# Order of the last products and of row tiles' turns, weight-block sums by accumulating transfers, and a bank for each half of the last product

## The chip, the cores and the metric

One core of one Trainium2 chip. The metric is the device time of one launch in microseconds, the median of several runs. TensorE (PE) multiplies, VectorE (DVE), ScalarE (ACT) and GpSimd (POOL) do the elementwise work, and transfers (DMA) are issued from SyncE's queue (SP) and from POOL's. Each engine executes its own list of instructions in order and waits on semaphores for the others.

## The reference

A decoder trunk of two layers over 512 tokens of width 1024, in float32:

```python
h = x
mix = gla_mixer(h, ...)                      # gated linear attention, ends in (..) @ gla_w_o, 1024 x 1024
h = layer_norm(ALPHA * h + mix, ln_g[0, 0], ln_b[0, 0])
h = layer_norm(ALPHA * h + relu(h @ mlp_w_up[0])**2 @ mlp_w_down[0], ln_g[0, 1], ln_b[0, 1])   # d_ff 4096
k, v = split(h @ kv_w)
mix = stick_breaking_attention(h @ sb_w_q[0], k, v) @ sb_w_o[0]
h = layer_norm(ALPHA * h + mix, ln_g[1, 0], ln_b[1, 0])
h = layer_norm(ALPHA * h + relu(h @ mlp_w_up[1])**2 @ mlp_w_down[1], ln_g[1, 1], ln_b[1, 1])
```

## The kernel before

**Precision and tiles.** Every float32 matrix is split into a rounded part hi (ScalarE, L70 and L98) and the rest lo (VectorE, L72 and L99), and every product is three matmuls, hi·hi, hi·lo and lo·hi. The 512 tokens are four row tiles of 128; the residual stream is four tiles `h300` to `h303` of 128 x 1024 (`hs`). Activations that are operands lie transposed in tiles `T` of 128 x 4 x 512 (8 buffers), weights in `raw` or `B` (8 buffers) and their splits in `hi` and `lo` (6 each). PSUM has 8 banks, `ps`. A bank that is written by TensorE and read by another engine is handed over as a whole.

**The seven-product stages.** `seven` multiplies a 512 x 1024 by a 1024 x 1024 block with seven half-size products in place of eight (Strassen-Winograd). It is used nine times: for `gla_w_o`, and four times in each MLP's down projection (g = 0, 2, 4, 6, named by the first of two 512-wide strips of d_ff). The left operand has quarters a11, a12, a21, a22 (views of two tiles), the right one b11 to b22, each as two halves `h`. `product` runs the two parts s = 0, 1 of a product (row tile s of the half; 12 matmuls of 512 columns each) and `add` adds a bank to the residual rows on VectorE. The sums on the a side, s1 = a22 - a21 (L332), s2 = -s1 - a11 (L334), a12 = -a12 - s2 (L340) and a21 = a11 - a21 (L341), are VectorE instructions of 1024 elements; b12 and b22 get their sums by a transfer from POOL's queue that adds in flight (`accum_op`), b11 and b21 by VectorE additions (L336 and L343), which overwrite the tile once its first use has been split. After the first products of the list come p3 (with b22 loaded anew), p7 and p4.

**Stages that end in a norm** (`norms=True`): `gla_w_o`, and g = 6 of both MLPs. There `seven` is a generator that gives control back when a row tile has all its sums. For each row tile VectorE takes statistics in pieces (L176), joins them (L180), adds epsilon (L183), POOL raises to the power -1/2 (`rs`, L185), VectorE centres the row (L189); then TensorE transposes it (the turn, L213), ScalarE applies the affine, and hi and lo are taken into the next stage's T tiles. `finish` does this and leaves the turns of the last row tiles to the next stage: `late` runs them in `up(0)`, the first strip of the next MLP, whose columns come in two halves of 256 (row tiles 0 and 1, then 2 and 3), or behind the first row tile of V. In the last stage of the program (`narrow=True`) nothing is turned: `done1` normalises each row tile (L202, L205) and stores it, and the last product, p4 of row tile 3, is made in two halves of 256 columns.

**What sets the order.** A scheduler takes the program as it is written and interleaves the engines' instructions by its own estimate; within an engine the order is then fixed. POOL's queue is in order, too: an accumulating transfer that waits for its tile holds up all that stands behind it there.

## Time and profile before

| | us |
|---|---|
| median of three runs (1152.15 to 1152.98) | 1152.26 |
| the profiled execution | 1151.73 |
| its span, first to last instruction | 1149.8 |
| TensorE busy | 1121.6 (98%) |
| VectorE busy | 821.0 (71%) |
| ScalarE busy | 555.3 (48%) |
| GpSimd busy | 141.9 (12%) |

The granted clock of TensorE was 0.995 over the span. A row of the timeline has the start in us from the span's start, the length in us, engine, line, operation, output and inputs, shape and count; in brackets the idle time of the engine ahead of it and what ended that. Lines are those of the kernel before (the changed kernel's lines are some 10 to 30 further down).

### The profile page before, as it was taken

What the parts mean: (1) busy time and instruction counts of PE and PEld (TensorE: products, weight loads), DVE (VectorE), ACT (ScalarE), POOL (GpSimd) and SP (SyncE); (2) the same over time, 40 slices, a digit from 0 to 9 for tenths busy, and PEclk for the clock granted to TensorE, in tenths of its full rate; (3) what the DMA queues carried; (4) which work ended last, traced back from release to release, by engine and by line L of the source; (5) the groups of instructions that cost most, each with busy time, mean ns of one, the idle gap of its engine ahead of it and who ended that gap; (6) DMA issues with size and microseconds to landing.
All of it is one profiled execution on the core that took longest, in us unless ns stands there. A gap on an engine that the chain in (4) does not pass through costs nothing.

```text
span 1149.8 us, 14087 instructions
## 1 busy us (share of the span) xinstructions
PE 1121.6 (98%) x5401; PEld 927.7 (81%) x5401; DVE 821.0 (71%) x1003; ACT 555.3 (48%) x823; POOL 141.9 (12%) x195
## 2 busy tenths in 40 slices
PE   8999999999999999999999999999999999999994
PEld 7788888798888888888788877778988888888883
DVE  4576648977757847759936878878667578467697
ACT  4454436654533535535725676754435335245360
POOL 1010110020000100100202434330100001001001
PEclk9999999999999999999999999999999999999998
DMA  7441291294670770831334221111945706708302
GB/s 232 127 116 50 75 247 63 75 300 138 170 215 19 199 204 19 217 95 37 110 110 129 58 71 53 58 37 37 298 142 161 224 19 186 209 27 203 90 1 73
DMA packets 97639, 140.73 MB, mean 122 GB/s; under 512 B 11874, under 2 KB 37602, under 8 KB 97572
## 3 DMA queue, kind: packets, MB, share of 16 engines
q1 hardware_dynamic: 87780, 120.96, 33.0%
q0 software_dynamic: 9792, 18.88, 9.3%
q8 instruction: 42, 0.69, 0.3%
q14 instruction: 25, 0.20, 0.1%
HBM read 137.72 MB, written 2.10 MB: 122 GB/s over the span
## 4 chain that ended last, share of the span: by engine, by line
PE 74%; DVE 19%; ACT 3%; issue 2%; POOL 1%; DMA 0%; SPq 0%; DVEq 0%; POOLq 0%; ACTq 0%
PE ps L318 22%; PE ps L93 17%; PE ps L94 16%; PE ps L95 16%; DVE lo L72 4%; DVE r L787 4%; DVE T L99 2%; DVE h L168 2%; ACT wt L802 1%; DVE bst L176 1%; ACT hi L70 1%; POOL rs L185 1%; DVE ps L779 1%; DVE h L189 1%; DVE qs L762 1%
## 5 line engine op out<-in xcount | busy, mean ns | idle before, releaser
L318 PE MATMUL ps<-hi,T 128*128 128x512 f32 (+1 forms) x1016 | 314.8, 389 | 8.2 <-DVE h L366 8.2
L93 PE MATMUL ps<-T,hi 128*128 128x512 f32 (+1 forms) x768 | 288.3, 376 | 1.7 <-ACT T L98 1.7
L94 PE MATMUL ps<-T,hi 128*128 128x512 f32 (+1 forms) x768 | 285.4, 372 | 0.0
L95 PE MATMUL ps<-T,lo 128*128 128x512 f32 (+1 forms) x768 | 285.4, 372 | 0.0
L72 DVE TENSOR_TENSOR lo<-raw,hi 128x1024 fp32r<-128x1024 f32 x134 | 163.0, 1226 | 125.0 <-ACT hi L70 124.1
L70 ACT ACTIVATE hi<-raw 128x1024 fp32r<-128x1024 f32 x134 | 142.7, 1066 | 181.1 <-PE ps L94 67.8
L318 PEld LDWEIGHTS ps<-hi,T 128*128 128x128 f32 x1016 | 191.1, 189 | 47.5 <-DVE h L366 8.4
L318 PE MATMUL ps<-lo,T 128*128 128x512 f32 (+1 forms) x508 | 197.4, 389 | 0.0
L72 DVE TENSOR_TENSOR lo<-B,hi 128x1024 fp32r<-128x1024 f32 x108 | 131.4, 1223 | 89.7 <-ACT hi L70 89.5
L70 ACT ACTIVATE hi<-B 128x1024 fp32r<-128x1024 f32 x108 | 114.2, 1058 | 160.1 <-PE ps L94 78.5
L93 PEld LDWEIGHTS ps<-T,hi 128*128 128x128 f32 x768 | 144.5, 188 | 26.7 <-ACT T L98 2.1
L95 PEld LDWEIGHTS ps<-T,lo 128*128 128x128 f32 x768 | 144.7, 188 | 25.2
L94 PEld LDWEIGHTS ps<-T,hi 128*128 128x128 f32 x768 | 144.8, 189 | 23.4
L318 PEld LDWEIGHTS ps<-lo,T 128*128 128x128 f32 x508 | 96.0, 189 | 19.4
L93 PE MATMUL ps<-hi,T 128*128 128x512 f32 x256 | 103.0, 403 | 0.0
L94 PE MATMUL ps<-lo,T 128*128 128x512 f32 x256 | 100.8, 394 | 0.1
L95 PE MATMUL ps<-hi,T 128*128 128x512 f32 x256 | 100.8, 394 | 0.0
L274 POOL DMA_DIRECT2D B<-in_mlp_w_down_dram x32 | 38.3, 1197 | 464.7 <-DMA B<-in_mlp_w_down_dram 420.5
L168 DVE TENSOR_TENSOR h<-h,ps 128x512 f32<-128x512 f32 x111 | 75.0, 679 | 10.9 <-PE ps L318 7.3
L787 DVE TENSOR_TENSOR_SCAN r<-r,begin 128x512 f32<-128x512 f32 x40 | 66.2, 1662 | 0.2
L788 POOL TENSOR_TENSOR w<-w,r 128x512 f32<-128x512 f32 x40 | 51.4, 1286 | 75.7 <-DVE r L787 60.4
L99 DVE TENSOR_TENSOR T<-s,T 128x1024 fp32r<-128x1024 f32 (+1 forms) x50 | 55.6, 1111 | 2.3 <-ACT T L98 2.3
(165 smaller groups left out, 1184.4 us busy)
## 6 DMA issues: line engine op xcount, KB each, us to landing
raw<-in_mlp_w_up_dram SPq DMA_DIRECT2D x64, 512.0 KB, 4.9
B<-in_mlp_w_down_dram SPq DMA_DIRECT2D x64, 512.0 KB, 5.7
B<-in_mlp_w_down_dram POOLq DMA_DIRECT2D x32, 512.0 KB, 8.7
raw<-in_gla_w_in_dram SPq DMA_DIRECT2D x20, 512.0 KB, 3.9
raw<-in_mlp_w_down_dram SPq DMA_DIRECT2D x16, 512.0 KB, 4.7
raw<-in_kv_w_dram SPq DMA_DIRECT2D x16, 512.0 KB, 4.0
B<-in_gla_w_o_dram SPq DMA_DIRECT2D x8, 512.0 KB, 8.5
raw<-in_sb_w_q_dram SPq DMA_DIRECT2D x8, 512.0 KB, 4.3
```

What stands on the lines that cost most here:

```text
L70: nc.scalar.activation(hi, raw, AF.Copy)
L72: nc.vector.tensor_tensor(lo, raw, hi.bitcast(F32), op=ALU.subtract)
L93: nc.tensor.matmul(ps, lhsT=a[0], rhs=b[0], start=first, stop=False)
L94: nc.tensor.matmul(ps, lhsT=a[0], rhs=b[1], start=False, stop=False)
L95: nc.tensor.matmul(ps, lhsT=a[1], rhs=b[0], start=False, stop=last)
L99: keep(nc.vector.tensor_tensor(lo, ps, hi.bitcast(F32), op=ALU.subtract))
L168: nc.vector.tensor_tensor(h, h, ps, op=op)
L176: nc.vector.bn_stats(out=self.st[:, parts * n + i, :], in_=h)
L274: nc.gpsimd.dma_start(out=to, in_=weights(more[0], h, more[1]), accum_op=ALU.add)
L318: nc.tensor.matmul(banks[s][:, c], lhsT=a(k, s)[x], rhs=b[k][y][:, c], start=opens and (k, x, y) == (0, 0, 0), stop=closes and (k, x, y) = ...
L787: nc.vector.tensor_tensor_scan(down, down, begins[kind][:, ::-1], 1.0, op0=ALU.mult, op1=ALU.max)
L788: nc.gpsimd.tensor_tensor(w, w, r[:, 1:S + 1], op=ALU.mult)
```

## The change

1. `finish` takes the generator itself. In the stages that turn rows, both parts of p3 come first, then both of p7, then both of p4 (before: p3 and p7 of one part, then of the other), and the generator says when a row has its sums (t) and when it is to be turned (~t). `late` is a list with one entry for each row: in `up(0)` row 2 is turned at piece k = 4 and row 3 at k = 5 (both at k = 4 before; where only row 3 is left, it comes at k = 5), and in V row 2 after the first row tile, row 3 after the second.
2. On the a side, a21 becomes a11 - a21 first, and its split for p7 (`seventh`) is made at once and kept; s2 = -a21 - a22, s1 = -s2 - a11 and a12 = -a12 - s2 follow from it. This is so in all nine stages; the number of VectorE instructions stays the same.
3. In the three stages that end in a norm, b11 and b21 get their sums by transfers: two more for each half of b11 and three for each half of b21, ten in a stage, instead of four VectorE additions.
4. In the last stage each half of the last p4 has a bank of its own.

```diff
-    def finish(mm, cols, hs, sp, work, turns=((), (0,), (1,), (2,))):
+    def finish(steps, cols, hs, sp, work):
...
-        for t in range(NT):
-            mm(t)
-            hs[t].stats()
-            hs[t].centre()
-            for q in turns[t]:
-                turn(q, work)
-        rest = [t for t in range(NT) if all(t not in q for q in turns)]
-        return lambda work: [turn(t, work) for t in rest]
+        rest = list(range(NT))
+        for t in steps:
+            if t < 0:
+                turn(~t, work)
+                rest.remove(~t)
+            else:
+                hs[t].stats()
+                hs[t].centre()
+        return [lambda work, t=t: turn(t, work) for t in rest]
...
-        tt(s1, a22, a21, op=ALU.subtract)
+        minus = lambda out, a, b: nc.vector.scalar_tensor_tensor(out, a, -1.0, b, op0=ALU.mult, op1=ALU.subtract)
+        tt(a21, a11, a21, op=ALU.subtract)
+        seventh = split_a(a21)
+        minus(s2, a21, a22)
+        minus(s1, s2, a11)
         third = split_a(s1), split_b(1)
-        nc.vector.scalar_tensor_tensor(s2, s1, -1.0, a11, op0=ALU.mult, op1=ALU.subtract)
-        for b22, b12, b11, b21 in bs:
-            tt(b11, b22, b11, op=ALU.add)
+        for h, (b22, b12, b11, b21) in enumerate(bs):
+            if norms:
+                more(b11, h, 0, 1)
+                more(b11, h, 1, 1)
+            else:
+                tt(b11, b22, b11, op=ALU.add)
...
-        for b22, b12, b11, b21 in bs:
-            tt(b21, b21, b11, op=ALU.add)
+        minus(a12, a12, s2)
+        for h, (b22, b12, b11, b21) in enumerate(bs):
+            if norms:
+                for k, j in ((0, 0), (0, 1), (1, 1)):
+                    more(b21, h, k, j)
+            else:
+                tt(b21, b21, b11, op=ALU.add)
...
-            yield
-            if not narrow:
+            yield s
+        if not narrow:
+            for s in range(2):
                 part(s, *p7, ys, False, False)
                 add(s, ys, 1, 1, last=True)
+                yield ~s
...
-                ps, hrow = bank(), hs[3]
                 for q in range(2):
                     c = slice(256 * q, 256 * q + 256)
-                    part(s, *p4, [None, ps], True, True, c)
+                    ps, h = [None, bank()], hs[3].h[:, c]
+                    part(s, *p4, ps, True, True, c)
...
-                    if g == 0 and (c0, k, f) == (0, 4, 0):
-                        late(work)
+                    if g == 0 and c0 == f == 0 and (k == 5 or k == 4 and len(late) > 1):
+                        late.pop(0)(work)
...
-            if (n, t) == (0, 0):
-                late(chain)
+            if late:
+                late.pop(0)(chain)
```

What this does to the engines' order is seen at three places. The first is VectorE in the last stage, from the first sum of the a side to the third product's split (`T1467` holds s1 and s2, `s21456` a12 and a22, `s21387` a11 and a21; `L99` makes a lo of the a side, `L72` a lo of a weight). Before:

```order
L332 TENSOR_TENSOR T1467_8845<-s21456_8812,s21387_8381 128x4x256
L168 TENSOR_TENSOR h300_1602<-h300_1602,ps1473_8857 128x512
L99 TENSOR_TENSOR T1475_8885<-s21456_8812,T1475_8885 128x4x256
L99 TENSOR_TENSOR T1480_8897<-T1467_8845,T1480_8897 128x4x256
L168 TENSOR_TENSOR h301_1603<-h301_1603,ps1474_8871 128x512
L334 SCALAR_TENSOR_TENSOR T1467_8845<-T1467_8845,s21387_8381 128x4x256
L72 TENSOR_TENSOR lo1491_8948<-B1461_8831,hi1490_8946 128x1024
L168 TENSOR_TENSOR h300_1602<-h300_1602,ps1485_8911 128x512
L99 TENSOR_TENSOR T1489_8943<-T1467_8845,T1489_8943 128x4x256
```

After:

```order
L168 TENSOR_TENSOR h300_1602<-h300_1602,ps1473_8869 128x512
L99 TENSOR_TENSOR T1475_8897<-s21456_8824,T1475_8897 128x4x256
L99 TENSOR_TENSOR T1480_8909<-s21387_8393,T1480_8909 128x4x256
L168 TENSOR_TENSOR h301_1603<-h301_1603,ps1474_8883 128x512
L343 SCALAR_TENSOR_TENSOR T1467_8857<-s21387_8393,s21456_8824 128x4x256
L72 TENSOR_TENSOR lo1492_8966<-B1461_8843,hi1491_8964 128x1024
L343 SCALAR_TENSOR_TENSOR T1467_8857<-T1467_8857,s21387_8393 128x4x256
L168 TENSOR_TENSOR h300_1602<-h300_1602,ps1486_8929 128x512
L72 TENSOR_TENSOR lo1494_8970<-B1465_8853,hi1493_8968 128x1024
L176 BN_STATS bst1487_8943<-h300_1602 128x6
L99 TENSOR_TENSOR T1481_8914<-T1467_8857,T1481_8914 128x4x256
```

The third product's operand was the first of these rows and its split the fourth (`T1480`); now the third row is the seventh product's split (`T1480` of the new program), the operand is made by two sums with a weight's lo between them, and its split (`T1481`) is the last row.

The second place is POOL's queue in that stage, behind the transfers that both kernels have (`B1461` and `B1465` are the halves of b11, `B1462` and `B1466` those of b21). Before:

```order
L274 DMA B1460_8828<-in_mlp_w_down_dram 128x2x512
L274 DMA B1463_8835<-in_mlp_w_down_dram 128x2x512
L274 DMA B1464_8838<-in_mlp_w_down_dram 128x2x512
L185 TENSOR_TENSOR rs1515_9067<-ve1514_9065,mhalf_73 128x1
L185 TENSOR_TENSOR rs1518_9095<-ve1517_9093,mhalf_73 128x1
L185 TENSOR_TENSOR rs1523_9140<-ve1522_9138,mhalf_73 128x1
```

After:

```order
L277 DMA B1464_8850<-in_mlp_w_down_dram 128x2x512
L277 DMA B1461_8843<-in_mlp_w_down_dram 128x2x512
L277 DMA B1465_8853<-in_mlp_w_down_dram 128x2x512
L277 DMA B1461_8843<-in_mlp_w_down_dram 128x2x512
L277 DMA B1465_8853<-in_mlp_w_down_dram 128x2x512
L277 DMA B1462_8845<-in_mlp_w_down_dram 128x2x512 x2
L277 DMA B1466_8855<-in_mlp_w_down_dram 128x2x512
L277 DMA B1462_8845<-in_mlp_w_down_dram 128x2x512
L277 DMA B1466_8855<-in_mlp_w_down_dram 128x2x512 x2
L185 TENSOR_TENSOR rs1515_9085<-ve1514_9083,mhalf_73 128x1
L185 TENSOR_TENSOR rs1518_9113<-ve1517_9111,mhalf_73 128x1
```

Ten transfers have come in ahead of the first row's power; those to one tile wait for one another.

The third place is the end of the program on VectorE, the last row tile. Before, and after:

```order
L366 TENSOR_TENSOR h303_1605<-h303_1605,ps1525_9167 128x256
L176 BN_STATS bst1524_9163<-h303_1605 128x6
L366 TENSOR_TENSOR h303_1605<-h303_1605,ps1525_9167 128x256
L176 BN_STATS bst1524_9163<-h303_1605 128x6
L180 BN_AGGR mv1526_9196<-bst1524_9163 128x2
L183 TENSOR_SCALAR ve1527_9198<-mv1526_9196 128x1
```

```order
L396 TENSOR_TENSOR h303_1605<-h303_1605,ps1525_9185 128x256
L396 TENSOR_TENSOR h303_1605<-h303_1605,ps1526_9200 128x256
L176 BN_STATS bst1524_9181<-h303_1605 128x6 x2
L180 BN_AGGR mv1527_9215<-bst1524_9181 128x2
L183 TENSOR_SCALAR ve1528_9217<-mv1527_9215 128x1
```

The second half has a bank of its own, `ps1526`, and its addition has moved ahead of the first half's statistics.

More of the change, by code (lines that the diff above doesn't have):

```diff
@@ L218, in turn_affine, with by_tiles @@
         put(sp.hi[u][:, :, c], sp.lo[u][:, :, c], y.rearrange("p (a b) -> p a b", a=4))
-    def finish(mm, cols, hs, sp, work, turns=((), (0,), (1,), (2,))):
+    def by_tiles(mm):
+        for t in range(NT):
+            mm(t)
+            yield t
+            if t > 0:
+                yield ~(t - 1)
+    def finish(steps, cols, hs, sp, work):
         def turn(t, work):
@@ L266, in seven, with more @@
         bs = []
+        def more(b, h, k, j):
+            nc.gpsimd.dma_start(out=b.rearrange("p (a b) -> p a b", a=2), in_=weights(k, h, j), accum_op=ALU.add)
         for h in range(2):
             four_b = []
-            for k, j, more in ((1, 1, (0, 1)), (0, 1, (0, 0)), (0, 0, None), (1, 0, None)):
+            for k, j, other in ((1, 1, (0, 1)), (0, 1, (0, 0)), (0, 0, None), (1, 0, None)):
                 b = pool.tile([P, 1024], F32, tag="B", bufs=8, name=nm("B"))
-                to = b.rearrange("p (a b) -> p a b", a=2)
-                nc.sync.dma_start(out=to, in_=weights(k, h, j))
-                if more:
-                    nc.gpsimd.dma_start(out=to, in_=weights(more[0], h, more[1]), accum_op=ALU.add)
+                nc.sync.dma_start(out=b.rearrange("p (a b) -> p a b", a=2), in_=weights(k, h, j))
+                if other:
+                    more(b, h, *other)
                 four_b.append(b)
@@ L349, in seven @@
             add(s, zs, 0, 1, last=True)
[L350 to L351 removed]
+            yield s
+        if not narrow:
+            for s in range(2):
                 part(s, *p7, ys, False, False)
                 add(s, ys, 1, 1, last=True)
+                yield ~s
         for s in range(2):
[L355 to L361 removed]
+            if not narrow:
+                part(s, *p4, ys, False, True)
+                add(s, ys, 1, 0, last=True)
+                yield 2 + s
+                continue
+            part(s, *p7, ys, False, True)
+            add(s, ys, 1, 1, last=True)
+            add(s, ys, 1, 0)
+            ys[s] = None
+            if s == 0:
+                part(s, *p4, ys, True, True)
+                add(s, ys, 1, 0, last=True)
+            else:
                 for q in range(2):
                     c = slice(256 * q, 256 * q + 256)
[L364 to L373 removed]
+                    ps, h = [None, bank()], hs[3].h[:, c]
+                    part(s, *p4, ps, True, True, c)
+                    tt(h, h, ps[1][:, c], op=ALU.add)
+                    hs[3].stat(0, q, h, 2)
+            yield 2 + s
     gl = tc.tile_pool(name="gla", bufs=1, reuse_waits="tile")
@@ L642, in yoco_kernel @@
     hT = Split()
-    late = finish(lambda t: next(steps), vcols, hs, hT, sgs, SEVEN)
+    late = finish(steps, vcols, hs, hT, sgs)
     op.__exit__(None, None, None)
@@ L694, in mlp @@
         steps = down(NG - 2, norms=True, narrow=l == 1)
-        got = done(lambda t: next(steps), work)
+        got = done(steps, work)
         ml.__exit__(None, None, None)
@@ L860, in part2, with done1 @@
             hs[t].add(n, pss[n], False, True)
-    late = finish(part2, vcols, hs, h3T, chain)
+    late = finish(by_tiles(part2), vcols, hs, h3T, chain)
     sbx.__exit__(None, None, None)
-    def done1(mm, work):
+    def done1(steps, work):
         vec = lnvec(1, 1)
@@ L869, in store @@
             nc.sync.dma_start(out=out2[128 * t:128 * t + 128, c], in_=hs[t].h[:, c])
-        for t in range(NT):
-            mm(t)
+        for t in steps:
             hs[t].stats()
```

23 lines of the change are left out of this document (3 added, 20 removed).

## The prediction

> **What bounds the kernel now.** I read the page first, then TensorE's waits, then the timeline at each of them. All times are of one profiled execution: it took 1151.73 us, of which the span is 1149.8; the three timed runs have a median of 1152.26, so a change worked out on the profiled execution is carried over to that median as a difference.
>
> ```profile
> span 1149.8 us, 14087 instructions
> PE 1121.6 (98%) x5401; PEld 927.7 (81%) x5401; DVE 821.0 (71%) x1003; ACT 555.3 (48%) x823; POOL 141.9 (12%) x195
> ...
> PE ps L318 <- DVE h L366: 8.2, 1, 8.2
> PE ps L213 <- DVE h L189: 3.8, 3, 2.0
> PE ps L93 <- ACT T L98: 1.7, 1, 1.7
> ```
>
> TensorE is busy for 98% of the span, and no edit takes a matmul away, so only its waits and the end can pay. The last three rows (total, times, longest) are the waits at places which the diff touches: 13.7 us together. Four of the five instructions behind them are:
>
> ```profile
> 224.60 0.74 PE L93 MATMUL ps<-T,hi 128*128 128x256 f32 x4 [1.67 <-ACT T L98]
> 226.19 0.76 PE L213 MATMUL ps<-ident,h 128*128 128x128 f32 x5 [0.84 <-DVE h L189]
> ...
> 566.97 1.09 PE L213 MATMUL ps<-ident,h 128*128 128x128 f32 x8 [2.01 <-DVE h L189]
> ...
> 809.06 0.66 PE L213 MATMUL ps<-ident,h 128*128 128x128 f32 x4 [0.93 <-DVE h L189]
> ```
>
> The reader is to see in the brackets the wait and its releaser: a row tile's transposes (L213) wait for its centring (L189), or the next matmul waits for a turned row tile (T). The fifth is at the end:
>
> ```profile
> 1130.52 0.28 PE L318 MATMUL ps<-hi,T 128*128 128x256 f32 x1
> 1138.96 0.58 PE L318 MATMUL ps<-hi,T 128*128 128x256 f32 x1 [8.15 <-DVE h L366]
> 1141.47 0.41 PE L318 MATMUL ps<-hi,T 128*128 128x256 f32 x1
> ...
> 1138.49 0.41 DVE L366 TENSOR_TENSOR h<-h,ps 128x256 f32<-128x256 f32 x1
> 1138.94 0.43 DVE L176 BATCH_NORM_STATS2 bst<-h 128x6 f32<-128x256 f32 x1
> 1141.92 0.42 DVE L366 TENSOR_TENSOR h<-h,ps 128x256 f32<-128x256 f32 x1 [2.56 <-PE ps L318]
> 1142.38 0.43 DVE L176 BATCH_NORM_STATS2 bst<-h 128x6 f32<-128x256 f32 x1
> 1142.84 0.26 DVE L180 BATCH_NORM_AGGREGATE mv<-bst 128x2 f32<-128x24 f32 x1
> ...
> 1096.00:1138.00 42.00, 34.80 (x160) 28.88 (x158) 42.00 (x62) 14.36 (x15) 2.76 (x3) 0.97 0.07 26
> ```
>
> The last row is a window by engine (length, then PE, PEld, DVE, ACT and POOL busy): VectorE has worked without a pause for the 42 us ahead of its add at 1138.49. So the 8.15 us on TensorE are not 8.15 us of the end. VectorE itself idles only the 2.56 us in which the second half is multiplied.
>
> **Own banks at the end.** With a bank for each half TensorE runs the second half right behind the first and is done some 1.5 us after 1130.8 (twelve 256-column matmuls, as from 1129.3 to 1130.8), about 6 us before VectorE gets there. VectorE then does add, add, statistics, statistics: four steps of 0.40 to 0.46 us by the rows above, 1.8 us, in place of 1142.84 - 1138.49 = 4.35. Gain 2.5 us; behind it the norm and the stores stay as they are. Bounds: 2.0 (if the second add still waits half a microsecond) to 2.6.
>
> **The turn of row 3 one step later, on the way to MLP 1.** It moves behind 12 matmuls of 256 columns, 12 x 0.12 = 1.4 us, more than the 0.93 it waits. Its centring depends on nothing that moved. Gain 0.9; bounds 0.6 to 0.93, since the second column half needs this row tile's split and comes 0.5 us sooner.
>
> **A longer chain on the a side, in all nine stages.** The third product's operand was one subtraction; now it is the last of three, and the seventh product's split comes ahead of it. In the last stage:
>
> ```profile
> 1096.09 1.23 DVE L332 TENSOR_TENSOR T<-s,s 128x1024 f32<-128x1024 f32 x1
> 1098.96 1.22 DVE L99 TENSOR_TENSOR T<-T,T 128x1024 fp32r<-128x1024 f32 x1
> 1100.10 0.68 DVE L168 TENSOR_TENSOR h<-h,ps 128x512 f32<-128x512 f32 x1
> 1103.57 1.06 ACT L70 ACTIVATE hi<-raw 128x1024 fp32r<-128x1024 f32 x1 [0.56 <-PE ps L318]
> 1104.50 0.62 PE L318 MATMUL ps<-hi,T 128*128 128x512 f32 x2
> 1104.96 0.39 PE L318 MATMUL ps<-lo,T 128*128 128x512 f32 x1
> ```
>
> Before, the sum stood at 1096.09 and its split was done 4.6 us before the third product began (1104.73, the second of the two matmuls of the row at 1104.50). By the new order the sums begin behind the add of 1100.10: sum, a weight's lo, sum, 3 x 1.14 us after 1100.3, is 1103.7. ScalarE is then in the hi of 1103.57, until 1104.6, and has the new hi at 1105.6. The lo follows on VectorE at 1107.2, but eight matmuls that need no lo of the a side stand in between, two of each of four half products, 8 x 0.23 = 1.8 us (0.46 for two by the last rows), which reach to 1107.4. So TensorE waits 0.9 us (0 to 1.9) in each of the three stages that end in a norm. In the last stage that costs nothing at the end: VectorE, which sets it, has one subtraction (1.14 us) fewer behind 1096, because a21's is made before, in idle time, and loses as much by waiting for the third product. In w_o the same count gives 0.9, too.
>
> In the other six stages I cost this at nothing; the cover is this slack:
>
> ```profile
> 383.30 1.22 DVE L99 TENSOR_TENSOR T<-T,T 128x1024 fp32r<-128x1024 f32 x1
> 386.79 0.62 PE L318 MATMUL ps<-hi,T 128*128 128x512 f32 x2
> ```
>
> The third product's split is done at 384.4 and the product starts at 387.0; the first product's T buffer, which the split must now wait for, is free before that. If the cover were gone, it would be up to 1 us for each of six.
>
> **Turns of rows 0 to 2.** These I walked by hand through the new order of both engines, with 1.14 us for a 1024-wide instruction of VectorE, 0.60 for a 512-wide one, 2.72 for a half product (12 x 0.227), 1.0 for eight transposes and 1.5 from a variance to the centring that needs its power:
>
> ```profile
> 225.32 0.81 DVE L189 TENSOR_SCALAR h<-h,mv,rs 128x1024 f32<-128x1024 f32 x1 [0.44 <-POOL rs L185]
> ...
> 235.58 0.68 DVE L195 TENSOR_TENSOR h<-h,lnb 128x512 f32<-128x512 f32 x1
> 236.18 0.68 DVE L99 TENSOR_TENSOR T<-s,T 128x512 fp32r<-128x512 f32 x1
> ```
>
> In w_o, rows 0 and 1 are finished ahead of p7's end and turned ahead of p4, so both gaps of 224.60 and 226.19 (2.5 us) go: I get row 1's centring at 217.1 where TensorE comes at 217.4, and row 2's at 228.9 where it comes at 229.7. Late next are row 3's centring (232.5, in time) and its split for the second column half, 238.5 against 237.9. Sum for w_o: -2.5 + 0.9 + 0.6 = -1.0; bounds -2.2 to +0.5. Before K and V, row 3's turn goes behind another row tile of V (24 x 0.23 = 5.5 us), so 2.0 goes. Against it stand the 0.9 and a new wait: rows 0 and 1 now have their statistics in one piece behind the last splits, row 0's centring ends at 551.8 and TensorE is there at 551.1. Sum -2.0 + 0.9 + 0.7 = -0.4; bounds -1.5 to +1.5. One thing is moved past here: row 3's power on POOL now stands behind the attention's fills.
>
> ```profile
> 564.30 1.38 POOL L185 TENSOR_TENSOR rs<-ve,mhalf 128x1 f32<-128x1 f32 x1
> 565.63 0.73 POOL L718 MEMSET begin<- 128x768 f32 x1
> ...
> 569.31 0.16 POOL L782 MEMSET r<- 128x1 f32 x3
> ```
>
> They take 3.9 us (565.63 to 569.5) and begin with row 1's last split, about 563.2; the power ends at 568.6, the centring at 569.9. TensorE comes at 571.6, so nothing is lost, but of 5.5 us only 1.7 are left.
>
> **Sums by transfers.** Four additions of 1.14 us leave VectorE in each of three stages. In the two MLP stages they stood in its idle time (1076 to 1086), so nothing is gained; in w_o two of them shorten a busy stretch in which it then waits for TensorE. In come 30 transfers, ten a stage, each adding 512 KB to a tile, one behind the other on a tile and all in POOL's order. In the last stage the first may start when the lo of b11 is made, and the last must have landed before the hi of the last b21:
>
> ```profile
> 1075.19 1.22 DVE L72 TENSOR_TENSOR lo<-B,hi 128x1024 fp32r<-128x1024 f32 x1
> 1115.87 1.06 ACT L70 ACTIVATE hi<-B 128x1024 fp32r<-128x1024 f32 x1 [0.30 <-PE ps L318]
> 1120.27 2.35 DVE L72 TENSOR_TENSOR lo<-B,hi 128x1024 fp32r<-128x1024 f32 x2
> ...
> L274 POOL DMA_DIRECT2D B<-in_mlp_w_down_dram x32: 1185/1198/1216, 234.3 to 1059.0; - x32
> B<-in_mlp_w_down_dram POOLq DMA_DIRECT2D x1, 512.0 KB, 5.9
> ...
> B<-in_mlp_w_down_dram POOLq DMA_DIRECT2D x2, 512.0 KB, 7.3
> ...
> B<-in_mlp_w_down_dram POOLq DMA_DIRECT2D x2, 512.0 KB, 9.8
> ...
> 1082.00:1096.00 14.00, 14.00 (x63) 11.59 (x63) 4.74 (x4) 7.83 (x11) 0.00 (x0) 1.00 0.00 0
> ```
>
> In POOL's new order five landings and two issues (1.20 us each) stand behind one another from 1076.3, where b11's second lo ends: 1078.7 + 5D. D, from issue to landing, was 5.9 us for one such transfer by itself (1034 to 1042), 7.3 for two some 2.7 us apart (315 to 329), 9.8 for two among 2.5 MB of loads (1055 to 1070). The chain ends at 1108.2, 1115.2 or 1127.7. The hi must be ready when VectorE reaches the last lo, at 1121.4, so the landing is due by 1120.3: D below 8.3. I take 7.3, because pairs overlap here and, by the last row, nothing else is moved (DMA share 0.00). Cost 0; bounds 0 and 7.4 us in this stage, the same in MLP 0, where the offset between the stages is constant, and in w_o, where three landings stand behind one another from 182.7 and 208 is the due time (D below 8.4), 0 and 4. What hides it is the slack of 5 us; gone, each microsecond is one of the end, as VectorE goes in order.
>
> [...]
>
> **Sum.** -2.5 - 0.9 - 1.0 - 0.4 + 0 = -4.8 us: the profiled execution from 1151.73 to 1146.9, the median from 1152.26 to 1147.5, or 0.42% less.
>
> **Rivals.** Chance in brackets; 0.2% (2.3 us) is what a measurement of this kernel can tell.
> The likeliest (0.55): the sum, 1147.5, own range 1146 to 1149.9.
> The chain of transfers is late (0.22): for it, D = 9.8 is in the same trace; against it, the quiet window. At D = 8.9 the landing is 3 us late in both MLP stages, +6 on the sum, 1153.5; from D = 9.1 (2 x 4 = 8 us, over 4.8 + 2.3 = 7.1) the kernel is slower. Half of it I give to no change, a little under half to slower.
> The new waits are larger (0.18): the third product waits 1.9 us, as it would without the interleaved matmuls, in w_o and MLP 0, and row 0's turn 1.5: +2.8, 1150.3, no change by a little.
> The whole 8.15 us come back (0.05): only if VectorE had slack before 1138.49, which the window excludes; 1142.
>
> Faster 0.65 (0.55, 0.05, and a part of the third), no change 0.24, slower 0.11. The range leaves out the very late chain and the whole 8 us: 1145.3 to 1153.
>
> **What would show it.** At the end TensorE without a wait between the two halves and VectorE's last aggregate about 2.5 us sooner; no wait above 1 us at L213; 0.9 us before the third product in three stages; on VectorE no wait for a hi of b21 near 1120, 544 and 209. A wait of the last lo for its hi, behind a landing, would make me wrong.

## The result and the profile after

The changed kernel takes 1144.39 us (median of four runs, 1143.0 to 1145.03) against 1152.2 before: ratio 0.9933, 95% interval 0.9916 to 0.995. A second series of five runs, beside other runs of the kernel before, gave 1143.94 and 0.9921 (0.9907 to 0.9934). The forecast was 1147.5 and the range began at 1145.3: the direction was right, the gain of 7.8 us was over 60% larger than the 4.8 forecast. One run of "one transfer more" below took 1878 us at a granted clock of 0.655 and is left out of its median.

The first lines to read are again TensorE's waits. In the list of waits (total, times, longest) of the changed kernel the places that the diff touches are now:

```profile
PE ps L329 <- ACT T L98: 2.3, 3, 0.8
...
PE ps L94 <- DVE T L99: 0.4, 1, 0.4
PE ps L213 <- DVE h L189: 0.2, 1, 0.2
```

13.7 us of waits have become 2.9. They stand in these rows of the timeline: the third product in w_o, in MLP 0 and in the last stage (L329 is `part`'s matmul, L318 before), row 3's split for the second column half, and row 1's turn before K and V.

```profile
193.45 0.50 PE L329 MATMUL ps<-hi,T 128*128 128x512 f32 x1 [0.83 <-ACT T L98]
237.12 0.39 PE L94 MATMUL ps<-T,hi 128*128 128x256 f32 x1 [0.38 <-DVE T L99]
526.86 0.50 PE L329 MATMUL ps<-hi,T 128*128 128x512 f32 x1 [0.74 <-ACT T L98]
551.12 0.55 PE L213 MATMUL ps<-ident,h 128*128 128x128 f32 x3 [0.15 <-DVE h L189]
1100.56 0.50 PE L329 MATMUL ps<-hi,T 128*128 128x512 f32 x1 [0.74 <-ACT T L98]
```

The end on VectorE, where before stood two adds 3.4 us apart:

```profile
1132.04 1.54 DVE L205 SCALAR_TENSOR_TENSOR h<-h,rs,lnb 128x512 f32<-128x512 f32 x3
1133.49 0.74 DVE L396 TENSOR_TENSOR h<-h,ps 128x256 f32<-128x256 f32 x2
1134.15 0.74 DVE L176 BATCH_NORM_STATS2 bst<-h 128x6 f32<-128x256 f32 x2
1134.93 0.26 DVE L180 BATCH_NORM_AGGREGATE mv<-bst 128x2 f32<-128x24 f32 x1
```

From the first add to the aggregate it is 1.44 us (1133.49 to 1134.93) in place of 4.35.

All kernels of this study have the same 5401 matmuls, so the start of the n-th one can be compared between two traces. The difference to the first profile of the kernel before is flat inside a stage and steps where something changed; that splits each profiled execution into five parts (us against the kernel before; "start" is up to 190 us, "w_o" 190 to 260, "MLP 0 to V" 500 to 600, "to MLP 1" 780 to 840, "end" from there to the last instruction). Between 260 and 500 nothing moved by more than 0.01 us in any kernel, and between the other parts by 0.1 at most.

| kernel | start | w_o | MLP 0 to V | to MLP 1 | end | median, us | ratio (95%) |
|---|---|---|---|---|---|---|---|
| changed | -1.01 | -1.48 | -1.78 | -0.82 | -3.44 | 1144.39 | 0.9933 (0.9916, 0.995) |
| changed, again | -0.20 | -1.45 | -1.76 | -0.82 | -3.38 | 1143.94 | 0.9921 (0.9907, 0.9934) |
| before, again | -0.09 | +1.15 | +1.62 | 0 | 0 | 1153.02 | 1.0003 (0.9993, 1.0013) |
| before + own banks | -1.64 | +1.03 | 0 | 0 | -2.90 | 1149.87 | 0.9976 (0.9965, 0.9986) |
| one bank | -1.31 | -1.40 | -1.77 | -0.82 | -0.49 | 1146.46 | 0.9946 (0.9932, 0.9959) |
| late turns together | -0.89 | -1.47 | +4.19 | 0 | -3.43 | 1149.35 | 0.9969 (0.9956, 0.9982) |
| products in pairs | -0.46 | -0.80 | -1.47 | -0.84 | -3.44 | 1144.84 | 0.9932 (0.9917, 0.9947) |
| sums on VectorE | -1.23 | -0.94 | -1.80 | -0.84 | -2.80 | 1144.82 | 0.9934 (0.9917, 0.995) |
| a side as before | -2.64 | -0.39 | -2.24 | -0.83 | -3.49 | 1144.01 | 0.9919 (0.9903, 0.9935) |
| third's split first | -0.12 | -0.94 | -2.84 | -0.83 | -3.93 | 1142.64 | 0.991 (0.9893, 0.9927) |
| one transfer more | -1.37 | -1.45 | -1.78 | -0.83 | -1.70 | 1143.53 | 0.9922 (0.9905, 0.9938) |
| third's first, not in w_o | +0.36 | -1.45 | -1.30 | -0.83 | -3.89 | 1142.36 | 0.9914 (0.99, 0.9928) |
| the two combined | -0.55 | -1.45 | -2.83 | -0.83 | -3.99 | 1141.87 | 0.9912 (0.9898, 0.9925) |

The parts behind the start repeat to 0.06 us for the changed kernel, the start itself scatters by 3 us over the fourteen profiles (the first of before stands at 0), and all of that arises in the first 15 us, far ahead of any edit. A median of five runs therefore tells less than the steps do, and below the steps decide. The change's own gain is -1.48 - 1.78 - 0.82 - 3.44 = -7.5 us.

### The profile page after: what moved, and what is told of

It reads as the page before. It is cut to its first block, busy times and chain, and to the rows that moved or that the text cites. A ratio compares the mean times of both kernels' runs of the same rounds, so it can differ in the third digit from the quotient of the medians.

```text
span 1141.3 us, 14137 instructions
## 1 busy us (share of the span) xinstructions
PE 1118.9 (98%) x5401; PEld 925.5 (81%) x5401; DVE 807.3 (71%) x991; ACT 554.5 (49%) x823; POOL 178.2 (16%) x225
## 4 chain that ended last, share of the span: by engine, by line
PE 78%; DVE 15%; ACT 3%; issue 2%; POOL 1%; DMA 0%; SPq 0%; DVEq 0%; POOLq 0%; ACTq 0%
PE ps L329 26%; PE ps L93 17%; PE ps L94 16%; PE ps L95 16%; DVE r L812 4%; DVE lo L72 3%; ACT wt L827 1%; DVE h L168 1%; DVE T L99 1%; DVE h L195 1%; DVE bst L176 1%; DVE ps L804 1%; ACT hi L70 1%; DVE qs L787 1%; POOL rs L185 1%
## 5 line engine op out<-in xcount | busy, mean ns | idle before, releaser
L329 PE MATMUL ps<-hi,T 128*128 128x512 f32 (+1 forms) x1016 | 314.2, 388 | 2.3 <-ACT T L98 2.3
L72 DVE TENSOR_TENSOR lo<-raw,hi 128x1024 fp32r<-128x1024 f32 x134 | 163.8, 1225 | 135.9 <-ACT hi L70 135.4
L329 PEld LDWEIGHTS ps<-hi,T 128*128 128x128 f32 x1016 | 190.2, 188 | 42.7 <-ACT T L98 4.1
L72 DVE TENSOR_TENSOR lo<-B,hi 128x1024 fp32r<-128x1024 f32 x108 | 131.1, 1222 | 93.8 <-ACT hi L70 93.6
L329 PE MATMUL ps<-lo,T 128*128 128x512 f32 (+1 forms) x508 | 196.9, 388 | 0.0
L277 POOL DMA_DIRECT2D B<-in_mlp_w_down_dram x52 | 62.4, 1230 | 539.5 <-DMA B<-in_mlp_w_down_dram 451.3
L329 PEld LDWEIGHTS ps<-lo,T 128*128 128x128 f32 x508 | 95.4, 188 | 19.2
L95 PEld LDWEIGHTS ps<-hi,T 128*128 128x128 f32 x256 | 48.3, 189 | 10.6 <-DVE T L99 0.3
```

The source lines that it names most:

```text
L72: nc.vector.tensor_tensor(lo, raw, hi.bitcast(F32), op=ALU.subtract)
L95: nc.tensor.matmul(ps, lhsT=a[1], rhs=b[0], start=False, stop=last)
L277: nc.gpsimd.dma_start(out=b.rearrange("p (a b) -> p a b", a=2), in_=weights(k, h, j), accum_op=ALU.add)
L329: nc.tensor.matmul(banks[s][:, c], lhsT=a(k, s)[x], rhs=b[k][y][:, c], start=opens and (k, x, y) == (0, 0, 0), stop=closes and (k, x, y) = ...
```

## The experiments

**Own banks alone.** On the kernel before:

```diff
-                ps, hrow = bank(), hs[3]
+                hrow = hs[3]
                 for q in range(2):
-                    c = slice(256 * q, 256 * q + 256)
+                    c, ps = slice(256 * q, 256 * q + 256), bank()
```

> The kernel before with one edit: each half of the last product's last row tile gets a bank of its own. Theory A (VectorE carries the end, and only its detour over TensorE between the two halves can be saved): the second half is multiplied right behind the first, and VectorE goes from its first add to the last aggregate in about 1.45 us in place of 4.35: 2.9 us less than the kernel before, about 1149.3; with 0.6 us more if the last stores also close faster, as in the changed kernel, 1148.7. Rival B (the whole wait of 8.15 us on TensorE comes back): about 1144. Rival C (the end's gain needs the changed kernel's sums too, because VectorE's own work ahead of it must shrink): no change by more than 0.5 us, 1152.

Theory A, to the hundredth: the end is 2.90 us shorter, not 8. The 0.6 us of the stores did not come with it (see the last section). The run also showed something that was not looked for: its w_o, which it shares word for word with the kernel before, took 1.03 us longer. That is taken up under "before, again".

**One bank again.** The changed kernel with this edit undone:

```diff
+                ps = [None, bank()]
                 for q in range(2):
-                    ps, h = [None, bank()], hs[3].h[:, c]
+                    h = hs[3].h[:, c]
```

> The changed kernel with one edit undone: the two halves of the last row tile share one bank again (its add and statistics stay in the new order, add and statistics of the first half ahead of the second half's add as far as the bank forces it). Theory A: the tail alone grows again, from the first half's add to the last aggregate by 2.9 us, all else as in the changed kernel: about 1147.3, that is 4.9 us less than the kernel before. Rival B (TensorE's 8 us wait is what costs): about 1151 to 1152. Rival C (the edits in the order of the a side had moved VectorE's last part too): the first add at another place than 45 us behind the stage's start.

The end grows by 2.95 us, and TensorE's wait returns almost whole:

```profile
1126.38 0.28 PE L329 MATMUL ps<-hi,T 128*128 128x256 f32 x1
1133.83 0.58 PE L329 MATMUL ps<-hi,T 128*128 128x256 f32 x1 [7.17 <-DVE h L397]
```

A wait of 7.17 us on the engine that is busy for 98% of the span is worth 2.9. The add at which VectorE arrives stands 0.1 us from where it stood in the kernel before, counted from the stage's start: rivals B and C fall.

**The a side in the order of before.** The reorder of the sums undone (a21's own difference stands behind a12's sum again, and its split for p7 behind that):

```diff
-        tt(a21, a11, a21, op=ALU.subtract)
-        seventh = split_a(a21)
-        minus(s2, a21, a22)
-        minus(s1, s2, a11)
+        tt(s1, a22, a21, op=ALU.subtract)
         third = split_a(s1), split_b(1)
+        minus(s2, s1, a11)
...
+        tt(a21, a11, a21, op=ALU.subtract)
```

> The changed kernel with the sums of the a side in the order of the kernel before (a22 - a21 first, from it the next; a21's own difference last). Theory A: the third product's waits of 0.84, 0.74 and 0.74 us in the three stages that end in a norm go, since its operand is one subtraction again; of these the ones in w_o and MLP 0 are worth the 1.6 us that they take on TensorE, the last stage's nothing at the end because VectorE carries it, but there a subtraction (1.14 us) comes back into VectorE's busy stretch, +0.3 to +1.1: in sum 0.5 to 1.3 us less than the changed kernel, 1143.1 to 1143.9. Rival B (the new order is what let the row tiles of w_o and MLP 0 be turned without a wait): a wait of about 1 us comes back at the turns of each of both stages, 1145 to 1147. Rival C: in the other six stages something waits, up to 1 us in each.

The third product's waits go in all three stages, as A says. In MLP 0 that is a gain of 0.46, and at the end it is nothing. In w_o rival B holds: 1.09 us are lost against the changed kernel, and the wait is at row 1's operands again:

```profile
221.78 0.74 PE L93 MATMUL ps<-T,hi 128*128 128x256 f32 x4 [1.04 <-ACT T L98]
222.80 0.39 PE L94 MATMUL ps<-T,hi 128*128 128x256 f32 x1 [0.28 <-DVE T L99]
```

By the steps this kernel is 0.6 us worse than the changed one; its median is equal within the scatter of the start.

**The third's split first.** One line moved behind the third's split, `seventh = split_a(a21)`.

> The changed kernel with one line moved: the seventh product's split is made behind the third's, not ahead of it. Theory A: the third product's operand comes one split (1.14 us of VectorE, and its hi on ScalarE) earlier, so its wait of 0.74 to 0.84 us in three stages goes; the seventh is needed much later and waits for nothing; w_o and MLP 0 gain 0.7 to 0.8 us each, the last stage nothing: 1.5 us less than the changed kernel, about 1142.9. Rival B (the third product's wait is set by ScalarE's hi of the weights, not by the a side's chain): the wait stays, 1144.4. Rival C (in the six other stages the third's split must wait for the first product's buffer, that the seventh took before): up to 1 us in each of six, 1146 to 1150.

Theory A in MLP 0 (-1.06 against the changed kernel) and, unlike A, also at the end: the wait is gone, and VectorE reaches the last row tile's add 1.06 us earlier from the stage's start. (0.55 of it is given back in the last stores, see the last section.) In w_o the wait stays, 0.84, as rival B says, but B's reason is not shown. The operand comes no earlier there: its last sum starts at 191.98 (191.09 in the changed kernel, whose start is 0.89 us shorter), since VectorE had made the seventh's split at 179.40, ahead of a wait for TensorE that has now grown from 0.34 to 1.46 us. ScalarE stands in order behind a weight's hi and is free at about the time at which that sum ends, so this does not tell which of the two holds the product up:

```profile
192.19 1.07 ACT L70 ACTIVATE hi<-raw 128x1024 fp32r<-128x1024 f32 x1 [3.00 <-PE ps L329]
193.24 2.96 ACT L98 ACTIVATE T<-T 128x1024 fp32r<-128x1024 f32 x3
194.35 0.50 PE L329 MATMUL ps<-hi,T 128*128 128x512 f32 x1 [0.84 <-ACT T L98]
```

Waits of 0.29 and 0.42 us come in behind it, and w_o loses 0.54. In sum 1.0 us better than the changed kernel. C did not occur.

**Late turns together.** `late` runs all that it holds at the earlier place (piece k = 4, or row tile 0 of V):

```diff
-                    if g == 0 and c0 == f == 0 and (k == 5 or k == 4 and len(late) > 1):
-                        late.pop(0)(work)
+                    if g == 0 and (c0, k, f) == (0, 4, 0):
+                        while late:
+                            late.pop(0)(work)
...
-            if late:
+            while late:
                 late.pop(0)(chain)
```

> The changed kernel with the late turns put back: the turns that were moved one step apart (row 3's behind another row tile, or behind another step) are made together again at the earlier place. Theory A (TensorE is in front of the centring there, and the later turn only covers this wait): the waits of about 2.0 us before K and V and 0.9 us on the way to MLP 1 come back, and perhaps 0.5 in w_o; 2.5 to 3.5 us more than the changed kernel by the stages of its profile, about 1147.2. Rival B (the centring has become early enough through the other edits, since POOL's power of rows 0 and 1 took 0.56 us and not 1.4): less than 1 us comes back, 1144.4 to 1145.4. Rival C (as B before K and V, but A on the way to MLP 1, where nothing else had moved): 0.8 us, 1145.2.

A in kind, but far larger: nothing in w_o, 0.82 on the way to MLP 1, and 5.97 us before K and V, where the kernel before had waited 2.0. TensorE there:

```profile
567.19 1.39 PE L213 MATMUL ps<-ident,h 128*128 128x128 f32 x8 [4.17 <-DVE h L189]
568.23 0.78 PE L93 MATMUL ps<-hi,T 128*128 128x512 f32 x1
568.81 0.63 PE L94 MATMUL ps<-lo,T 128*128 128x512 f32 x1
569.23 0.63 PE L95 MATMUL ps<-hi,T 128*128 128x512 f32 x1
```

A window of 3 us behind the wait, by engine (length, PE, PEld, DVE, ACT and POOL busy, granted clock):

```profile
568.00:571.00 3.00, 3.00 (x10) 2.42 (x9) 2.98 (x6) 3.00 (x9) 0.00 (x0) 0.50 0.16 47
```

4.17 are the wait. The matmuls behind it follow each other by 0.43 us, where the undisturbed ones take 0.227, at a granted clock of 0.50; these make the other 1.8 us. Why 4.17 and not 2.0: this trace is 2.36 us ahead of the kernel before when the stage begins (its start and w_o), and counted from there TensorE is at the turn 0.4 us later (563.0 against 565.0, start less wait), but the centring begins 3.0 us later (566.3 against 565.7). In the new order VectorE makes a weight's lo and row 2's centring between row 3's last add (557.69) and its statistics (560.85); the variance then stands behind another lo that waits for ScalarE, and POOL can only begin behind that:

```profile
563.99 1.23 DVE L72 TENSOR_TENSOR lo<-raw,hi 128x1024 fp32r<-128x1024 f32 x1 [1.23 <-ACT hi L70]
565.13 0.15 DVE L183 TENSOR_SCALAR ve<-mv 128x1 f32<-128x1 f32 x1
...
565.37 0.92 POOL L185 TENSOR_TENSOR rs<-ve,mhalf 128x1 f32<-128x1 f32 x1 [0.15 <-DVE ve L183]
566.32 0.81 DVE L189 TENSOR_SCALAR h<-h,mv,rs 128x1024 f32<-128x1024 f32 x1 [0.45 <-POOL rs L185]
```

**Products in pairs.** p3 and p7 of one part, then of the other, and the turns of rows 0 to 2 where they were, all else as changed:

```diff
             yield s
-        if not narrow:
-            for s in range(2):
+            if not narrow:
+                if s == 1:
+                    yield ~0
                 part(s, *p7, ys, False, False)
                 add(s, ys, 1, 1, last=True)
-                yield ~s
...
                 yield 2 + s
+                if s == 0:
+                    yield ~1
```

> The changed kernel with the last products in pairs by row half again (third and seventh of one row half, then of the other), and the turns of rows 0 to 2 at the places of the kernel before. Theory A (the order of the products is what gives the row tiles their time): in w_o the two waits of 1.67 and 0.85 us return, with the third product's 0.8 kept, so w_o is 1.5 to 2.5 us slower than in the changed kernel; before K and V row 0's statistics come earlier, so its 0.15 us wait goes, but the gap ahead of row 1 and the restarts come back, +0.3 to +1; the last stage is unchanged. In sum 1146.2 to 1147.9. Rival B (the sums by transfers gave VectorE the time in w_o): w_o keeps at least 1 us of its gain of 1.5 us, 1144.4 to 1145.2.

Both theories missed. The waits of 1.67 and 0.85 do not return; waits of 0.47 and 0.61 stand at w_o's turns instead. The order of the products, with the turns that go with it, is worth 0.68 us in w_o and 0.31 before K and V: less than half of w_o's gain, so A is too large, and more than B left to it. That the median lies in B's range is the scatter of medians: by the steps this kernel is 1.0 us worse than the changed one.

**Sums on VectorE.** `tt(b11, b22, b11)` and `tt(b21, b21, b11)` for all stages, and no further transfer that adds.

> The changed kernel with the sums of the weight blocks b11 and b21 on VectorE again in the three stages that end in a norm (four additions of 1.14 us a stage, and no transfer that adds). Theory A (in both MLP stages the additions stand in VectorE's idle time, in w_o partly in a busy stretch): the MLP stages as in the changed kernel to 0.3 us, w_o 0 to 1.2 us longer; 1144.4 to 1145.6. Rival B (the sums by transfers are what lets VectorE reach the last row tiles sooner): VectorE's add of the last row tile comes 2 to 4.6 us later behind the start of the last stage, the span grows by as much, 1146.4 to 1149. Rival C (the transfers cost by their landing or by their issue on POOL): it is faster than the changed kernel by more than 0.5 us, below 1143.9.

Theory A: the MLP stages keep their times (0.02; at the end the add of the last row tile is at the same place to 0.01, and the 0.64 that are lost lie in the last stores). W_o loses 0.54. So 20 of the 30 transfers buy nothing in these runs.

**One transfer more.** To measure the slack of the chain in the last stage:

```diff
-                for k, j in ((0, 0), (0, 1), (1, 1)):
+                for k, j in ((0, 0), (0, 1), (1, 1)) + ((1, 1),) * (narrow and h == 1):
```

> The changed kernel with one adding transfer more (512 KB) on the second half of b21 in the last stage alone, behind the other three on this tile; the sum in this tile is another than the reference's, all else is the same. Theory A (the transfers of one tile follow one another by a landing each, 5.8 to 6.2 us): the last packets end at about 1117 in place of 1111, the hi of that half starts that much later, VectorE waits 1 to 2 us before the last lo, and the end is 1 to 2 us later: 1145.4 to 1146.4. Rival B (the transfers of one queue overlap, so one more costs its packets only, 3.6 us): the landing is at about 1114.5 and nothing waits: 1144.4. Rival C (TensorE waits, too, since the half's products stand in line, 2 to 4 us more at the end): 1147 to 1149.

Theory A, with the wait at the place the prediction had named for a late chain:

```profile
1116.67 1.06 ACT L70 ACTIVATE hi<-B 128x1024 fp32r<-128x1024 f32 x1 [5.50 <-DMA B<-in_mlp_w_down_dram]
...
1117.76 1.22 DVE L72 TENSOR_TENSOR lo<-B,hi 128x1024 fp32r<-128x1024 f32 x1 [1.65 <-ACT hi L70]
```

The end part of the profiled execution is 1.74 us longer than in the changed kernel, and TensorE waits for nothing more. So the chain had some 4.5 us to spare in the last stage: one landing more (6.2 us, the row of the ten transfers further down) is too much by 1.7. (The sum in this tile is wrong by the transfer that was added; the kernel only serves to measure time.) The median does not show this (1143.53); only the profiled execution, at 1144.36, is known to have waited.

**The third's split first, but not in w_o.**

```diff
+        if norms and fresh:
+            seventh = split_a(a21)
         minus(s2, a21, a22)
         minus(s1, s2, a11)
         third = split_a(s1), split_b(1)
-        seventh = split_a(a21)
+        if not (norms and fresh):
+            seventh = split_a(a21)
```

> The changed kernel with the third product's split ahead of the seventh's in eight of the nine stages; w_o keeps the changed kernel's order. Theory A (each stage keeps the gain that it showed by itself: w_o 1.48 us as in the changed kernel against 0.94 with the third first; MLP 0 to the attention 2.84 and the last stage 3.9 as with the third first): 9.1 us less than the kernel before by the stages from w_o on, 0.5 less than with the third first everywhere, 1.5 less than the changed kernel: about 1142.6. Rival B (w_o's 0.5 us between the two orders was the scatter of one profile): w_o as with the third first, 0.94, and a median equal to that kernel's.

W_o as A says (-1.45). But MLP 0, whose instructions are those of the kernel with the third's split first, took 1.54 us longer than there. The last hi of b21, the last lo and row 0's turn tell why:

```profile
543.45 1.06 ACT L70 ACTIVATE hi<-B 128x1024 fp32r<-128x1024 f32 x1 [5.26 <-DMA B<-in_mlp_w_down_dram]
...
544.55 1.22 DVE L72 TENSOR_TENSOR lo<-B,hi 128x1024 fp32r<-128x1024 f32 x1 [1.40 <-ACT hi L70]
...
550.51 1.09 PE L213 MATMUL ps<-ident,h 128*128 128x128 f32 x8 [0.98 <-DVE ve L183]
```

And the transfers of that stage, the ten that add and three plain loads beside them (KB each, median us from issue to landing), of this kernel and then of the one with the third's split first:

```profile
B<-in_mlp_w_down_dram POOLq DMA_DIRECT2D x10, 512.0 KB, 7.5
raw<-in_kv_w_dram SPq DMA_DIRECT2D x3, 512.0 KB, 4.5
```

```profile
B<-in_mlp_w_down_dram POOLq DMA_DIRECT2D x10, 512.0 KB, 6.2
raw<-in_kv_w_dram SPq DMA_DIRECT2D x3, 512.0 KB, 3.7
```

This is the prediction's rival of the late chain, in one execution: all transfers of the stretch landed a fifth later, the hi came after its time, and VectorE passed the delay on to the turns of rows 0 and 1.

**The same two kernels again.**

> The changed kernel unchanged, to have its profile and times a second time beside the others. Theory A (the stages repeat, and only the start differs from run to run): w_o 1.48, MLP 0 to the attention 1.78, the attention 0.82 and the last stage 3.44 us less than in the first profile of the kernel before, each to 0.1 us, while the time up to w_o differs by up to 1 us. Rival B (w_o's gain, too, is a matter of the run): w_o differs by 0.3 us or more.

> The kernel before unchanged, a second profile. [...]

The changed kernel repeats to 0.06 us in each part (A). The kernel before does not: this time w_o is 1.15 and "MLP 0 to V" 1.62 us longer, with the same waits in the same places. The windows behind the two waits, in the second profile and then in the first one (length, busy times, granted clock third from the end):

```profile
226.00:229.00 3.00, 2.91 (x16) 2.84 (x17) 3.00 (x6) 1.33 (x3) 0.00 (x0) 0.64 0.51 167
568.00:571.00 3.00, 2.97 (x11) 2.69 (x12) 3.00 (x5) 3.00 (x9) 2.35 (x9) 0.53 0.56 183
```

```profile
226.00:229.00 3.00, 2.81 (x23) 2.74 (x24) 3.00 (x6) 1.37 (x3) 0.00 (x0) 1.00 0.53 171
567.00:570.00 3.00, 3.00 (x18) 2.62 (x19) 3.00 (x5) 3.00 (x9) 2.29 (x9) 1.00 0.62 198
```

Sixteen matmuls and transposes against 23 in the same 3 us, and 11 against 18 in the other 3 us: behind waits of 1.67 and 0.85, and of 2.01 us, the matmuls ran at about half the rate in this execution (in w_o 256-column matmuls start 0.21 us apart at a granted clock of 0.64) and at the full one in the profile that I predicted from (0.12 us apart at 1.00). "Own banks alone" had it in w_o (0.53 from 225 to 228) and not before V (1.00 from 566 to 574). So the 1.0 us that "own banks alone" lost in w_o need not be its edit's: the kernel before loses as much in one execution and not in the other. Before V, where I had looked for no difference, the same holds behind the one wait.

**The two combined.** The sums of both MLP stages on VectorE (`if norms and fresh:` ahead of the `more` calls; both hold in w_o alone), and the third's split first except in w_o.

> The changed kernel with two edits, each limited to where the stages showed a gain: in both MLP stages the sums of the weight blocks are VectorE's again (the transfers that add stay in w_o alone), and the third product's split is ahead of the seventh's in all stages but w_o. Theory A (the transfers are worth 0.5 us in w_o and nothing in the MLP stages, where they were once 1.5 us late; the third product's wait is worth 1.06 us in MLP 0 and as much at the end): w_o 1.5, MLP 0 to the attention 2.8, the attention 0.8 and the last part 3.9 to 4.5 us less than the kernel before, in sum 9.0 to 9.7; median about 1142.3, with no run made longer by a late landing. Rival B (with VectorE's four additions in the same stage the earlier split is not reached sooner): the third product's wait of 0.74 us is back in both MLP stages, as in the changed kernel, 1144. Rival C (the additions push the last row tile's work back, as VectorE is now the bound without a wait for the third product): up to 1 us at the end, 1143.3.

Theory A in every part. 1141.87 is the lowest median of the study: 10.4 us under the kernel before in the same series, and 1.6 us under the changed kernel by the parts behind the start.

## Why the prediction was right or wrong

Behind the start the steps gave 7.5 us where 4.8 were forecast. Of the 2.7 that the forecast left out, 1.4 are before K and V, 0.9 at the end (0.6 of them in the last stores) and 0.5 in w_o; the turn on the way to MLP 1 gave 0.1 less than forecast. The waits that were to go did go. What failed is the size of these three terms, of the one before K and V above all, which with the end's term came out beyond its own bound (-1.5 and 2.6).

**Own banks (2.5 forecast, 2.9 measured, 3.44 with the stores).** The mechanism held: VectorE carries the end, and only its detour counts. The size was off: I took 0.40 to 0.46 us for each of four steps, from rows in which each one needs the one ahead. Back to back on separate halves two adds start 0.33 us apart and the four steps take 1.44, not 1.8. The other 0.6 stand behind the last L205 and no step of mine had them.

**The turn one step later (0.9; 0.82).** Right, and undoing it gave 0.82 back.

**The longer chain (0.9 in three stages; 0.83, 0.74, 0.74).** Right, also that it costs nothing in the other six and nothing at the end. That last zero was two things that cancel: a subtraction out of the busy stretch, 1.14, against VectorE's waits for the third product. "The third's split first" shows the two apart: without the wait the add comes 1.06 sooner.

**Turns in w_o (-1.0; -1.48).** Both gaps are gone and the split for the second half is late, at 0.38 instead of 0.6. The rest, about 0.2, are the waits under 0.13 us and the slower first matmuls behind each break (behind the wait at 237.12 the second starts 0.22 us after the first, the ones that follow 0.12 us apart), which I had left out. The working put the whole gain on the order of the products. The runs show that to be 0.68 of it; taking away the new a side costs 1.09 and taking away the transfers 0.54. These add up to 2.3, more than the gain, so the edits' shares overlap: some of the time is saved only as several come together.

**Turns before K and V (-0.4; -1.78).** The step that failed is "1.5 from a variance to the centring that needs its power". It was taken from rows in which POOL's power took 1.4 us, and it takes 0.56 as often. Before and then after, row 0's power and what VectorE does beside it:

```profile
549.62 1.40 POOL L185 TENSOR_TENSOR rs<-ve,mhalf 128x1 f32<-128x1 f32 x1 [66.75 <-DVE ve L183]
549.38 1.22 DVE L72 TENSOR_TENSOR lo<-raw,hi 128x1024 fp32r<-128x1024 f32 x1
```

```profile
547.20 0.56 POOL L185 TENSOR_TENSOR rs<-ve,mhalf 128x1 f32<-128x1 f32 x1 [17.46 <-DVE mv L180]
547.08 0.64 DVE L176 BATCH_NORM_STATS2 bst<-h 128x6 f32<-128x512 f32 x1
```

In w_o and before V, in the profiles of the kernel before and the changed one, it takes 0.54 to 0.57 us beside statistics, beside an add from a bank or beside nothing, and 1.38 to 1.40 beside a weight's lo; beside the affine of L195 it took 0.92 in "late turns together" (565.37). In the new order row 0's power falls beside statistics. From the variance (546.90) to the centring (547.79) it is 0.9 us there and not 1.5, and row 0's turn comes without the forecast wait of 0.7:

```profile
547.79 0.81 DVE L189 TENSOR_SCALAR h<-h,mv,rs 128x1024 f32<-128x1024 f32 x1
...
548.78 1.04 PE L213 MATMUL ps<-ident,h 128*128 128x128 f32 x8
```

That is 0.55 of the 1.4 us that this term lacks, as 0.15 us of waiting are left of the 0.7. They stand at row 1's turn, whose power is beside a lo again (1.40). This is read from the rows; no run changes the power's neighbour alone. The third product waited 0.74 and not 0.9. Of the remaining 0.7 us some 0.3 are waits of about 0.1 that are gone; the other 0.4 are no idle time in the profile and are put down to slower restarts behind the waits (at 526.86 the second matmul starts 0.34 us after the first, the next 0.24 after that); this is an estimate and was not taken apart. Row 3's power did land behind the fills, as forecast: it started at 565.07 and TensorE came at 568.18, and "late turns together" shows what the later turn covers, 6 us and not the 2 that the kernel before waited there.

**Sums by transfers (0).** Right in both MLP stages. In w_o they are worth 0.54; there two of the four additions stand in a busy stretch, which I had named and not priced, and whether those two are the reason was not taken apart. The transfers of the last stage on POOL, where the next issue stands behind a landing (at 1080.27 and 1089.08 two issues are in one row):

```profile
1072.17 1.20 POOL L277 DMA_DIRECT2D B<-in_mlp_w_down_dram  x1 [0.53 <-DVE lo L72]
...
1080.27 2.44 POOL L277 DMA_DIRECT2D B<-in_mlp_w_down_dram  x2 [2.22 <-DMA B<-in_mlp_w_down_dram]
1089.08 2.46 POOL L277 DMA_DIRECT2D B<-in_mlp_w_down_dram  x2 [6.38 <-DMA B<-in_mlp_w_down_dram]
...
1098.57 1.20 POOL L277 DMA_DIRECT2D B<-in_mlp_w_down_dram  x1 [1.78 <-DMA B<-in_mlp_w_down_dram]
1105.08 1.20 POOL L277 DMA_DIRECT2D B<-in_mlp_w_down_dram  x1 [5.30 <-DMA B<-in_mlp_w_down_dram]
...
B<-in_mlp_w_down_dram POOLq DMA_DIRECT2D x10, 512.0 KB, 6.2
```

The last row is the median of all ten, 6.2 against the 7.3 that I took. But the five landings that stand behind one another took 7.8, 7.3, 8.5, 6.2 and 5.7, 7.1 in the mean, so 7.3 was the right size for the chain: it ended at 1110.8, which is 1115.9 in the kernel before's time (this trace is 5.06 us ahead of it), against 1115.2 by the working. The 4.5 us that "one transfer more" found to spare agree with the due time of 1120.3. The rival, a late chain at chance 0.22, is a real one: it came in one of the nine profiled executions that have these transfers in MLP 0. There the five landings took 8.1 in the mean, near the 8.3 that I had as the limit. About 1.06 of the 1.4 us that VectorE waited are that kernel's own, as it reaches this lo earlier; the changed kernel would have lost some 0.3 by that count, so its limit in MLP 0 is about 8.0. That "the offset between the stages is constant" was taken and not read.

The issues on POOL took 1198 ns at the median in both kernels. The longest after, 1.73 us at 1089.81 and 1.69 us at 505.18 and 514.06, each began 0.73 us behind another issue; VectorE began a lo within 0.1 us of two of them and did nothing beside the third. So these rows do not tie the length of an issue to what VectorE runs.

**Range.** Its low end left out that several terms could be better at once, and it took the profiled execution for the kernel before as a whole. That execution had no half-rate matmuls behind its waits in w_o and before V (granted clock 1.00 in the 3 us behind each); the second profile of the same program had 2.8 us of them. The timed runs have no profile, but the granted clock that is on record for each points to most of them: of 55 runs of the kernel before beside these experiments 37 had 0.989 to 0.993 and a median of 1153.3 us, the other 18 had 0.994 or 0.995 and 1151.4. All 42 runs of the kernels without the long waits in w_o and before K and V had 0.994 to 0.996. A run's clock holds its start as well, so this is a hint and not a count; it does not enter the -7.5 above, to which such an execution would add up to 2.8.

## What to carry to other kernels

A wait on the busiest engine is worth what the engine at the end of the chain loses by it (7.2 us were worth 2.9 here), and a turn's later place is worth the wait that it would have now, not the one of the kernel before (6.0 against 2.0). Price a step between two engines by what its neighbour runs beside it (POOL's power took 0.56 us beside statistics and 1.40 beside a weight's lo), and compare two traces by the n-th matmul: steps of 0.1 us become readable where medians scatter by two. Work moved to transfers that add in flight was free here with five landings of 7.1 us in the mean behind one another, and not with 8.1 (MLP 0, one execution, where VectorE waited 1.40 us for the hi); put it where it buys time, and leave it out where VectorE is idle.

## What the runs showed of the hardware

**The clock behind short waits.** Waits of 1.67 and 0.85 us, 0.75 us apart, left the granted clock of the next 3 us at 1.00 in one profile of the kernel before and at 0.64 in another; a wait of 2.01 us left 1.00 or 0.53; after 4.17 us it was 0.50. Where it fell, the price was 1.0 to 1.8 us. The length of the wait alone does not tell which: 2.0 us were followed by the lower clock in one profile of three.

**The last stores.** From the end of the last L205 to the end of the program it is 3.74 us in the kernel before and 3.15 after, and this goes with neither edit: 3.75 with own banks alone, 3.15 with one bank. SyncE's last three issues take, before, after, and with the sums on VectorE:

```profile
1145.30 1.58 SPq L869 DMA_DIRECT2D out_dram<-h  x3
```

```profile
1137.39 1.30 SPq L894 DMA_DIRECT2D out_dram<-h  x3
```

```profile
1137.65 1.56 SPq L886 DMA_DIRECT2D out_dram<-h  x3
```

In the trace's record SyncE pauses 0.34 us ahead of the 464th instruction of its queue, in the nine profiles in which the queue does not wait there anyway, and just as long ahead of the 336th and the 208th: 128 instructions apart. With 479 to 482 instructions in all the 464th is among the last three issues; with 483 it falls where the queue waits 3.2 us or more for VectorE, and with 486 among an earlier row tile's stores, where there is time. The close is 3.64 to 3.78 us in the seven profiles of the first kind and 3.14 to 3.16 in the seven others. So the changed kernel's 0.6 us go with its one instruction more than before, in all fourteen profiles; no run changes the number of instructions alone. The three issues above account for 0.3 of the 0.6, and what the pause is stays open.
